# One-hot expert rows copied by ScalarE to a layout with each token's keys contiguous, for the gate matmuls' stationary side

## The chip, the core and the metric

The kernel runs on one core of a Trainium2 chip. The engines named here are TensorE (PE, whose weight loads the profile lists apart as PEld), VectorE (DVE), ScalarE (ACT), GpSimd (POOL) and SyncE (SP, which issues the large loads). Each engine works off its own instructions, and waits for others through semaphores. The metric is the device time of the whole program in microseconds (us).

## The reference, cut to what matters

A token batch of 256 rows of 1024 channels passes four layers. The first two of them (attention and others, not touched here) each end in a PEER feed-forward block, which chooses among 16,384 experts, laid out as 128 x 128 keys:

```python
def peer_ffn(h, w_pq, sub_keys, expert_down, expert_up):
    ...
        s = jnp.einsum('thpk,hpnk->thpn', q, sub_keys, ...)
        top_s, top_i = lax.top_k(s, PEER_TOPK)                     # 16 of 128, two lists per head
        ...
        best_s, best_pos = lax.top_k(cand_s..., PEER_TOPK)         # 16 experts for each of 8 heads
        gate = jax.nn.softmax(best_s, axis=-1)
        u = expert_down[experts]
        act = jax.nn.gelu(jnp.einsum('td,thkd->thk', t, u, ...))
        wgt = (gate * act).astype(t.dtype)
        return jnp.einsum('thk,thkd->td', wgt, expert_up[experts])
```

## The kernel before

The kernel gathers no experts. In `peer` it computes the activations of all 16,384 experts for all 256 tokens, multiplies them by a dense matrix of gates that is zero for experts not chosen, and multiplies the result by the whole up table.

**Units.** The down table comes as 64 loads of 1 MB, two units each, and a unit is 128 experts (one row of the 128 x 128 keys). For each unit `Stream.next` has ACT make a float32r high part (`whi`, L95, one CAST of 128x1024) and DVE the remainder (`wlo`, L100, one TENSOR_TENSOR of 128x1024); then PE runs 24 matmuls of 128x256 (`mtile`, L226). A pool holds three pairs of `whi` and `wlo`, so the cast for a unit waits until PE is through with the unit three before it. The split is written in the program two units ahead of its matmuls. After every second unit ACT applies GELU to the pair before (L971, and L974 with a product on DVE, L975, for the tokens whose gates are there already).

**Gates.** The generator `peer_select` is stepped between units by a debt counter: every unit is worth 1400, a step costs what it yields. Its first part finds the chosen experts of every token. Its second part, the **gate stage**, goes through the tokens four at a time, 64 groups per layer. The tile `w6` holds two sets `O` of three float16 planes of 128 keys x 4 tokens, the token index running fastest, so that two keys of a token lie 8 bytes apart. For a group, DVE compares a ramp with the row and column numbers of the chosen experts (L924, one-hot rows in plane 0, one-hot columns in plane 2), and one step later multiplies the one-hot columns by the two float16 parts of the gates (L928, planes 1 and 2). The contraction index on the partitions is the list of 128 chosen pairs. `gate_mm` then runs 8 matmuls of 128x128 for the group: plane 0 of a token is the stationary side, planes 1 and 2 are the moving side, and the results are the token's 128 x 128 gates in a bank of PSUM. `evac` takes an older group's bank: ACT copies the gates for the experts whose activations are still to come (L901, one or two pieces), and DVE multiplies them into the activations that are there (L904). In the program order a group is L924, a yield of 800, `evac`, L928, the matmuls of the group before, a yield of 800.

Nothing reorders the work: each engine's instructions stand in the order in which this Python code emits them. In the profile all matmuls carry L226, and the tiles `w` (w6), `bank` (PSUM), `arena` and `a` (activations, `a` also other scratch), `r` (loaded weights), `hthi` and `htlo` (the tokens) tell them apart. L888 are four float16 transposes, whose stationary and moving side both lie contiguous.

Of the kernel before, what the change touches and what calls it, by code (L numbers as in the profile page):

```python
# [12 lines left out]
OP = mybir.AluOpType  # L13
# [7 lines left out]
# columns of the per-channel vectors, [128, count] each  # L21
# [10 lines left out]
class Stream:  # L32
    """Loads run ahead in one queue, in the order of use; tiles of weights are split into two
    float32r parts a few units before they are needed."""
# [36 lines left out]
    def mark(self):  # L71
        """nothing behind this place is split before it is passed"""
        self.todo.append((None, None, None))
# [44 lines left out]
    def raw_due(self, ahead=0):  # L118
        """the next raw item was loaded in front of the tiles in use, or not far behind"""
        return self.raw_q and self.raw_q[0][2] < self.at + ahead  # L120


class Kern:
# [16 lines left out]
    def __init__(self, nc, tc, ctx, a, out):  # L140
        self.nc, self.tc, self.ctx, self.a, self.out = nc, tc, ctx, a, out
        P = lambda name, **kw: ctx.enter_context(tc.tile_pool(name=name, **kw))
        self.perm = P("perm", bufs=1)
        self.hl = P("hl", bufs=3)
        self.htp = P("ht", bufs=1)
        self.ps = P("ps", bufs=8, space=PSUM)
        self.sm = P("small", bufs=1)
        p = self.perm
        self.arena = p.tile([128, 26624], F32, name="arena")
        self.x = p.tile([128, 8, 256], F32, name="x")  # L150
        self.vec = p.tile([128, NVEC], F32, name="vec")
        self.ident = p.tile([128, 128], F32, name="ident")
        self.ones = p.tile([128, 128], F32, name="ones")
        self.adac = [p.tile([128, 48], F32, name=f"adac{i}") for i in range(4)]
        self.gs = p.tile([128, 8], F32, name="gs")
        self.epst = p.tile([128, 1], F32, name="epst")
        self.one = p.tile([128, 1], F32, name="one")
        self.zo = p.tile([128, 8], F32, name="zo")
        self.z2 = p.tile([128, 20], F32, name="z2")
        self.zr = p.tile([128, 1], F32R, name="zr")  # L160
        self.ident16 = p.tile([128, 128], F16, name="ident16")
        self.io4 = p.tile([128, 128, 4], F16, name="io4")
        # parts that change to float32r where the experts come
        self.rp = P("rp", bufs=1)
        self.a3 = self.rp.tile([128, 6144], F32, name="a3")
        self.r0 = self.rp.tile([128, 4096], F32, name="r0")
        self.r0s = [self.r0[:, :2048], self.r0[:, 2048:]]
        self.w6 = self.rp.tile([128, 1536], F32, name="w6").rearrange("p (a b) -> p a b", b=256)
        self.w6_at = 0
        self.late = False  # L170
        self.S = Stream(self, 2)
        self.slots = [self.arena[:, i * 2048:(i + 1) * 2048] for i in range(13)]
        self.ring = list(range(2, 10))
        self.reset()

# [12 lines left out]
    def reset(self, lo=20480):  # L188
        """scratch: parts of the arena that the loads leave alone"""
# [4 lines left out]
    def second(self):  # L194
        """from here on other tiles of scratch serve, and the loads have eight places"""
# [11 lines left out]
    def rounded(self):  # L207
        """float32r tiles for the experts"""
        self.a3 = None
        self.fa3 = self.rp.tile([128, 6144], F32R, name="fa3", tag="a3")  # L210
# [22 lines left out]
    def mtile(self, o, h):  # L233
        """o[128 outputs, 256 tokens] from the next unit of weights and h (d on partitions)."""
        hi, lo = self.S.next()
# [5 lines left out]
    def mtile2(self, os, h, lead=None):  # L241
        """two tiles at once, as the blocks of h come"""
# [39 lines left out]
    def gemv(self, l, m, cb, pool=0):  # L282
        """columns m, m + 1 of layer l's modulation, from the next raw item, without their bias"""
# [32 lines left out]
    def sq_mm(self, sq, ss, col, cols=8):  # L316
        """column sums of sq [128, 256], tokens on partitions, into columns col, cols + col"""
# [4 lines left out]
    def sums(self):  # L322
        """opens the sums of squares of x, tokens on partitions"""
# [4 lines left out]
    def sum_mm(self, sq, ss, k):  # L328
        """adds block k's squares [128, 256]"""
# [11 lines left out]
    def warm(self, n):  # L341
        """keeps the tensor engine's clock up while it would wait"""
# [5 lines left out]
    def warm_root(self):  # L348
        """has the table of the square root loaded"""
        self.nc.scalar.activation(self.one, self.epst, AF.Sqrt)  # L350

    def root(self, parts, n, d):
        """1 / sqrt(mean + eps) for the sums over the last axis of parts [128, n, ...]"""
# [6 lines left out]
    def spread(self, r):  # L360
        """r: for both blocks of tokens a column -> [128, 256], the same on all partitions"""
# [5 lines left out]
    def rstd(self, ss, r=None):  # L367
        """for both blocks of tokens a column of 1 / rms"""
# [6 lines left out]
    def norm(self, r, g, sc, sh, keep=None):  # L375
        """hi, lo of x * rstd * g * (1 + sc) + sh"""
# [25 lines left out]
    def lead(self, cb):  # L402
        """the first norm, two blocks at a time as the columns of their scale and shift come"""
# [31 lines left out]
    def x_step(self, ps, k, g, ss):  # L435
        """block k of x and its squares, whose sums the caller takes later"""
# [5 lines left out]
    def out_open(self):  # L442
        """x += g * (w_out^T h) with the channels of h in any order: four banks stay open"""
# [4 lines left out]
    def out_step(self, h, k, g=None):  # L448
        """one block of 128 channels of h; with g it is the last"""
# [29 lines left out]
    def add_mixer1(self, l, ada, every):  # L479
        """ada: pairs of modulation columns, their loads between those of the weights"""  # L480
# [15 lines left out]
    def mixer1(self, l, h, g, lead=None):  # L496
# [7 lines left out]
        # q and k, channels on partitions; heads c and c + 4 share a tile  # L504
# [47 lines left out]
        # v and the gating half, tokens on partitions  # L552
# [10 lines left out]
        # normalised q, k  # L563
# [46 lines left out]
        # y holds the three branches: attention 0..3, convolution 4..5, gating 6..7  # L610
# [79 lines left out]
        # group norm of the gating half  # L690
# [62 lines left out]
    def act(self, jp):  # L753
        """two activations of every token"""
# [3 lines left out]
    def up_order(self, i):  # L758
        """pairs whose room goes to the loads come first"""
# [3 lines left out]
    def add_peer_up(self, l, extra):  # L763
        """extra: modulation columns (layer, m0, n) whose loads go between"""
# [11 lines left out]
    def top16(self, src, n, val, idx, tmp):  # L776
        """top 16 of each row of src [128, cnt, n]; a generator, one step per row pair"""
# [19 lines left out]
    def peer_select(self, qT, keys, st):  # L797
        """top experts of every token and head -> gates and indices with the pairs on partitions,
        then the gate matrix of every token, multiplied into the activations."""
# [31 lines left out]
        for tb in range(2):  # L831
# [16 lines left out]
            # softmax over the 16 best, in two float16 parts of gate * 2^15  # L848
# [10 lines left out]
            # place among the candidates -> places in the two lists  # L859
# [31 lines left out]
        # gate matrices  # L891
# [18 lines left out]
        def gate_mm(O, t0):  # L910
            ps = self.bank()
            for t in range(4):
                o = ps[:, t * 128:(t + 1) * 128]
                self.mm(o, O[:, 0, :, t], O[:, 1, :, t], True, False)
                self.mm(o, O[:, 0, :, t], O[:, 2, :, t], False, True)
            pend.append((ps, t0))

        for t0 in range(0, 256, 4):
            # one-hot rows and columns, the columns times the gate's parts
# [4 lines left out]
            TX(O[:, 0::2], io, bc(0), op=OP.is_equal)  # L924
# [13 lines left out]
    def peer(self, l, h, g2, extra):  # L938
# [16 lines left out]
        # the arena is the activations' from here on  # L955
# [40 lines left out]
        # up: tokens stationary, the table moving  # L996
# [76 lines left out]
    def gla(self, h, g):  # L1073
# [16 lines left out]
        # decay  # L1090
# [22 lines left out]
        # values, tokens on partitions  # L1113
# [52 lines left out]
        def states(hd):  # L1166
            """the state after every chunk"""
# [96 lines left out]
    def softplus(self):  # L1264
        """8 softplus(-lambda) and its negative"""
# [23 lines left out]
    def lru(self, h, g):  # L1289
# [28 lines left out]
        def wgate(w, o, bn, b):  # L1318
            """a gate of half b, block-diagonal"""
# [141 lines left out]
    def route(self, h, hf, ht):  # L1461
        """combine weights, one-hot groups and ranks of the tokens inside their group"""
# [10 lines left out]
        # the tokens, rows  # L1473
# [23 lines left out]
        # top two of each group of four  # L1497
# [9 lines left out]
        # the first group with the largest sum  # L1507
# [8 lines left out]
        # tokens of the same group in front of each token; their count after the last  # L1516
# [6 lines left out]
        # rank inside the group, ties to the lower index  # L1523
# [35 lines left out]
    def experts(self, S, base, ht, w, oh, rk, g2, r, first=None, lent=()):  # L1559
        """slots base..base+127 of every group through the group's four experts"""  # L1560
# [19 lines left out]
        def gather(g2_):  # L1580
            """the tokens of two groups"""
# [46 lines left out]
        def turn(e):  # L1628
            """the hidden rows of expert e, channels on partitions"""
# [97 lines left out]
    def moe(self, l, h, hf, g2):  # L1727
# [22 lines left out]
        # groups of more than 128 tokens: their other slots  # L1750
# [14 lines left out]
def build(nc, tc, ctx, a, out, upto=99):  # L1765
# [7 lines left out]
    # modulation columns that load while the experts' second table does  # L1773
    extra = [[(0, 40, 8, "c"), (1, 0, 48, "c"), (2, 0, 24, "c2")], [(2, 24, 24, "c2"), (3, 0, 48, "c2")]]

    # the order of every load of the program
# [76 lines left out]
def _mtiles(w):  # L1853
    """[1024, N] -> [N / 256, 128, 2 * 1024]: two tiles of 128 outputs to a load."""
# [5 lines left out]
def arrays_of(inputs):  # L1860
# [39 lines left out]
    # modulation, [4 layers, 24, 128, 2 * 1024]  # L1900
    ada = np.stack([f["w_ada"][0], f["w_ada"][1], f["ada_w_2"][0], f["ada_w_2"][1]])
    A["ada"] = c(ada.transpose(0, 2, 1).reshape(4, 24, 2, 128, 1024).transpose(0, 1, 3, 2, 4).reshape(4, 24, 128, 2048))
    # attention bias by distance
# [72 lines left out]
```

## Time and profile before

| | |
|---|---|
| median of 3 runs | 2842.04 us (2841.47 to 2843.13) |
| profiled execution, from its first to its last instruction | 2840.8 us |
| PE busy | 2758.2 us (97%) |
| DVE busy | 2309.9 us (81%) |
| ACT busy | 1566.3 us (55%) |
| mean DMA rate | 232 GB/s |

The profiled execution has no clock but its own span, 2840.8 us, which is 1.2 us under the median of the timed runs. Busy time is a sum over stages with different limits. The gate stages lie from about 374 to 641 us (first layer) and 1329 to 1596 us (second layer) of the span, and their own rows tell what limits them.

### The profile page before, as it was taken

The page shows a single profiled execution, that of the slowest core. Times are in us where ns is not written, and L with a number is a line of the kernel's source. Part 1 is how long each engine was busy: PE and PEld are TensorE (multiplying, and loading weights), DVE is VectorE, ACT ScalarE, POOL GpSimd, SP SyncE. Part 2 cuts the span into 40 slices and gives each one's busy share as a digit, 9 for nine tenths or more (in the row PEclk, how much of TensorE's full clock was granted, in tenths as well). Part 3 has the DMA queues.
Part 4 walks back from the last instruction along what each step waited for, and adds up shares of the span by engine and source line. Part 5 has one row for each costly group of instructions (what it writes and reads, how often), then busy time and mean ns, then how long its engine had stood idle before and what let it go on. Part 6 is the DMA issues. An engine that isn't in the chain of part 4 may idle for free. (4 is left out here: it accounts for less than half of the span.)

```text
span 2840.8 us, 43874 instructions
## 1 busy us (share of the span) xinstructions
PE 2758.2 (97%) x17371; PEld 2485.0 (87%) x17371; DVE 2309.9 (81%) x3701; ACT 1566.3 (55%) x2250; POOL 68.1 (2%) x60
## 2 busy tenths in 40 slices
PE   6899999999999999999999999999999999989998
PEld 5799999998888889999999888888888887978886
DVE  7858988896788866698789868887479997779997
ACT  4554454434544445455444454455567786767785
POOL 3400000000000000000000000000000000000000
PEclk9899999999999989999999999999999999999998
DMA  9461544445899943335444479986249998359894
GB/s 379 187 239 58 173 164 142 142 148 198 334 405 359 334 169 136 125 120 177 135 149 136 172 260 371 357 337 227 90 161 358 342 349 303 135 184 364 326 361 159
DMA packets 93751, 658.09 MB, mean 232 GB/s; under 512 B 10932, under 2 KB 12468, under 8 KB 14808
## 3 DMA queue, kind: packets, MB, share of 16 engines
q1 hardware_dynamic: 90432, 649.44, 62.0%
q10 hardware_dynamic: 3096, 5.68, 0.6%
q8 instruction: 140, 2.29, 0.3%
q14 instruction: 83, 0.68, 0.1%
HBM read 654.03 MB, written 1.05 MB: 231 GB/s over the span
## 5 line engine op out<-in xcount | busy, mean ns | idle before, releaser
L100 DVE TENSOR_TENSOR wlo<-arena,whi 128x1024 fp32r<-128x1024 f32 x610 | 734.6, 1221 | 229.3 <-ACT whi L95 216.7
L226 PE MATMUL bank<-hthi,whi 128*128 128x256 f32 x2920 | 851.4, 292 | 17.7 <-ACT whi L95 9.5
L95 ACT CAST whi<-arena 128x1024 fp32r<-128x1024 f32 x610 | 631.7, 1044 | 386.0 <-PE bank L226 375.6
L226 PE MATMUL bank<-htlo,whi 128*128 128x256 f32 x2920 | 834.9, 286 | 4.0 <-DVE htlo L386 2.5
L226 PE MATMUL bank<-hthi,wlo 128*128 128x256 f32 x2920 | 833.3, 285 | 4.8 <-DVE wlo L100 4.7
L95 ACT CAST whi<-r 128x1024 fp32r<-128x1024 f32 x331 | 347.8, 1051 | 527.3 <-PE bank L226 514.6
L226 PEld LDWEIGHTS bank<-hthi,whi 128*128 128x128 f32 x2920 | 566.3, 194 | 30.7 <-ACT whi L95 9.8
L226 PE MATMUL bank<-whi,hthi 128*128 128x512 f32 (+1 forms) x1472 | 573.3, 389 | 2.4 <-ACT hthi L265 2.4
L226 PEld LDWEIGHTS bank<-htlo,whi 128*128 128x128 f32 x2920 | 565.1, 194 | 10.2 <-DVE htlo L386 7.9
L226 PE MATMUL bank<-wlo,hthi 128*128 128x512 f32 (+1 forms) x1472 | 571.3, 388 | 0.5 <-DVE wlo L100 0.5
L226 PE MATMUL bank<-whi,htlo 128*128 128x512 f32 (+1 forms) x1472 | 571.5, 388 | 0.2
L226 PEld LDWEIGHTS bank<-hthi,wlo 128*128 128x128 f32 x2920 | 563.9, 193 | 6.3 <-DVE wlo L100 6.1
L100 DVE TENSOR_TENSOR wlo<-r,whi 128x1024 fp32r<-128x1024 f32 x331 | 404.9, 1225 | 152.9 <-ACT whi L95 150.9
L226 PEld LDWEIGHTS bank<-whi,hthi 128*128 128x128 f32 x1472 | 276.4, 188 | 58.4 <-ACT hthi L265 2.8
L226 PEld LDWEIGHTS bank<-whi,htlo 128*128 128x128 f32 x1472 | 276.3, 188 | 57.5 <-DVE htlo L266 1.1
L226 PEld LDWEIGHTS bank<-wlo,hthi 128*128 128x128 f32 x1472 | 276.4, 188 | 56.4 <-DVE wlo L100 1.2
L292 DVE SCALAR_TENSOR_TENSOR arena<-arena 128x1024 f32<-128x1024 f32 x136 | 163.6, 1240 | 0.0
L226 PE MATMUL bank<-w 128*128 128x128 f16 x1024 | 142.0, 296 | 1.3 <-DVE w L928 1.3
L226 PE MATMUL bank<-whi,fw 128*128 128x512 f32 x360 | 121.8, 392 | 1.7 <-ACT fw L265 1.5
L904 DVE SCALAR_TENSOR_TENSOR arena<-bank,arena 128x416 f32<-128x416 f32 (+23 forms) x128 | 123.3, 963 | 0.0
L100 DVE TENSOR_TENSOR fa<-arena,fa 128x1024 fp32r<-128x1024 f32 x96 | 117.5, 1224 | 5.2 <-ACT fa L95 0.3
L95 ACT CAST fa<-arena 128x1024 fp32r<-128x1024 f32 x96 | 101.0, 1052 | 27.0 <-PE bank L226 26.7
(341 smaller groups left out, 2815.3 us busy)
## 6 DMA issues: line engine op xcount, KB each, us to landing
r<-in_pdown SPq DMA_DIRECT2D x110, 1024.0 KB, 4.8
arena<-in_pup SPq DMA_DIRECT2D x81, 1024.0 KB, 6.6
arena<-in_ada SPq DMA_DIRECT2D x72, 1024.0 KB, 7.0
arena<-in_mg SPq DMA_DIRECT2D x64, 1024.0 KB, 5.8
arena<-in_mu SPq DMA_DIRECT2D x64, 1024.0 KB, 6.0
arena<-in_md SPq DMA_DIRECT2D x64, 1024.0 KB, 6.4
r<-in_pup SPq DMA_DIRECT2D x47, 1024.0 KB, 5.7
r<-in_ada SPq DMA_DIRECT2D x24, 1024.0 KB, 6.8
```

The lines of the kernel that those rows point to most:

```text
L95: k.nc.scalar.copy(hi[:, :n], ap)
L100: self.k.nc.vector.tensor_sub(lo[:, :n], ap, hi[:, :n].bitcast(F32))
L226: self.nc.tensor.matmul(o, l, r, start=start, stop=stop)
L292: self.nc.vector.scalar_tensor_tensor(w, w, 1.0, cb, op0=OP.mult, op1=OP.mult, accum_out=o)
L904: nc.vector.scalar_tensor_tensor(o[:, :, :j - j0], p4[:, :, j0:j], 1.0 / GSC, o[:, :, :j - j0], op0=OP.mult, op1=OP.mult)
```

## The change

The one-hot rows now go to plane 1 and the columns stay in plane 2 (one TENSOR_TENSOR as before, its output now contiguous). ScalarE copies plane 1 to plane 0 and swaps the two axes, so that there each token's 128 keys lie contiguous. The gate matmuls take their stationary side from this copy. The moving side is read as before, 8 bytes from key to key. L928 overwrites plane 1, so it comes after the copy.

```diff
         def gate_mm(O, t0):
             ps = self.bank()
             for t in range(4):
                 o = ps[:, t * 128:(t + 1) * 128]
-                self.mm(o, O[:, 0, :, t], O[:, 1, :, t], True, False)
-                self.mm(o, O[:, 0, :, t], O[:, 2, :, t], False, True)
+                row = O[:, 0].rearrange("p j t -> p (j t)")[:, t * 128:(t + 1) * 128]
+                self.mm(o, row, O[:, 1, :, t], True, False)
+                self.mm(o, row, O[:, 2, :, t], False, True)
             pend.append((ps, t0))

         for t0 in range(0, 256, 4):
...
-            TX(O[:, 0::2], io, bc(0), op=OP.is_equal)
+            TX(O[:, 1:3], io, bc(0), op=OP.is_equal)
+
+            nc.scalar.copy(O[:, 0].rearrange("p j t -> p (j t)").rearrange("p (t j) -> p t j", t=4),
+                           O[:, 1].rearrange("p j t -> p t j"))
             yield self.GC
             if len(pend) == 2:
                 evac(*pend.popleft())
             TX(O[:, 1:3], O[:, 2:3].to_broadcast([128, 2, 128, 4]), bc(2), op=OP.mult)
             if last is not None:
                 gate_mm(*last)
```

The new file also leaves out comments and docstrings. In it the comparison is L925, the copy L927, the product L932, and L971, L974 and L975 become L975, L978 and L979.

What ACT has to do in the first layer where about half of the activations are there (which the trace of before runs from 439.7 us on), before; `r` holds the loaded weights, and the words in brackets are the semaphores that a row waits for:

```order
L95 CAST whi<-r_93 128x1024 [waits DVE_49,PE_49]
L971 ACTIVATE arena<-bank 128x2x204
L974 ACTIVATE gt<-bank 128x2x52 [waits DVE_49]
L901 ACTIVATE arena<-bank 128x4x34
L901 ACTIVATE a_92<-bank 128x4x24
L95 CAST whi<-r_93 128x1024 [waits DMAHW2_49,PE_49]
L901 ACTIVATE arena<-bank 128x4x34
L901 ACTIVATE a_92<-bank 128x4x24
```

The same place now:

```order
L927 COPY w_94<-w_94 128x512 [waits DVE_49,Activation_49]
L95 CAST whi<-r_93 128x1024
L975 ACTIVATE arena<-bank 128x2x204
L978 ACTIVATE gt<-bank 128x2x52 [waits Activation_49]
L901 ACTIVATE arena<-bank 128x4x34
L901 ACTIVATE a_92<-bank 128x4x24
L95 CAST whi<-r_93 128x1024 [waits DMAHW2_49,PE_49]
L927 COPY w_94<-w_94 128x512 [waits DVE_49,Activation_49]
L901 ACTIVATE arena<-bank 128x4x34
L901 ACTIVATE a_92<-bank 128x4x24
```

A copy (L927) stands ahead of a cast at the first place and ahead of the two pieces of an evacuation (L901) at the second, and each waits for DVE. Over the 64 groups of a layer, 37 copies have a cast right behind them and 27 an L901; outside the gate stages ACT's order is as it was.

DVE at the same place now:

```order
L925 TENSOR_TENSOR w_94<-io_88,TT 128x1024 [waits PE_49]
L100 TENSOR_TENSOR wlo<-r_93,whi 128x1024 [waits Activation_49]
L979 TENSOR_TENSOR arena<-arena,gt 128x2x52 [waits Activation_49]
L904 SCALAR_TENSOR_TENSOR arena<-bank,arena 128x4x70 [waits Activation_49]
L932 TENSOR_TENSOR w_94<-w_94,TT 128x1024 [waits DVE_49]
L100 TENSOR_TENSOR wlo<-r_93,whi 128x1024 [waits DMAHW2_49,PE_49,Activation_49]
L925 TENSOR_TENSOR w_94<-io_88,TT 128x1024 [waits PE_49]
L904 SCALAR_TENSOR_TENSOR arena<-bank,arena 128x4x70 [waits Activation_49]
L932 TENSOR_TENSOR w_94<-w_94,TT 128x1024 [waits DVE_49]
```

Its order is that of before (there the comparison is L924 and the product L928). Both the remainder (L100) and the evacuation (L904) wait for ACT, as they did; what has moved is what stands ahead of that on ACT.

## Rows read from the trace of the kernel before

**Rows 1.** The page's first part: busy us, share, instructions.

```profile
PE 2758.2 (97%) x17371; PEld 2485.0 (87%) x17371; DVE 2309.9 (81%) x3701; ACT 1566.3 (55%) x2250; POOL 68.1 (2%) x60
```

**Rows 2.** Busy time by engine in both gate stages: stretch, its length, PE, PEld, DVE, ACT, POOL, clock, DMA.

```profile
374.48:640.79 266.31, 266.31 (x2231) 262.93 (x2229) 227.49 (x308) 119.16 (x249) 0.00 (x0) 1.00 0.43 147
1329.50:1595.85 266.35, 266.35 (x2231) 262.95 (x2229) 227.45 (x308) 119.14 (x249) 0.00 (x0) 1.00 0.43 147
```

**Rows 3.** Waits in the first gate stage: us in total, times, longest.

```profile
ACT whi L95 <- PE bank L226: 145.4, 71, 2.6
DVE wlo L100 <- ACT whi L95: 30.8, 35, 1.9
DVE w L924 <- PE bank L226: 7.3, 16, 0.8
```

**Rows 4.** Timeline of DVE in the first gate stage: start, us, instruction.

```profile
440.79 0.69 DVE L924 TENSOR_TENSOR w<-io,TT 128x1024 f16<-128x1024 f16 x1 [0.71 <-PE bank L226]
441.40 1.22 DVE L100 TENSOR_TENSOR wlo<-r,whi 128x1024 fp32r<-128x1024 f32 x1
...
444.63 1.23 DVE L100 TENSOR_TENSOR wlo<-r,whi 128x1024 fp32r<-128x1024 f32 x1 [0.51 <-ACT whi L95]
445.77 0.69 DVE L924 TENSOR_TENSOR w<-io,TT 128x1024 f16<-128x1024 f16 x1
446.37 0.79 DVE L904 SCALAR_TENSOR_TENSOR arena<-bank,arena 128x280 f32<-128x280 f32 x1
447.08 0.68 DVE L928 TENSOR_TENSOR w<-w,TT 128x1024 f16<-128x1024 f16 x1
```

**Rows 5.** Timeline of ACT in the same stretch.

```profile
439.72 1.05 ACT L95 CAST whi<-r 128x1024 fp32r<-128x1024 f32 x1 [2.27 <-PE bank L226]
...
443.54 1.05 ACT L95 CAST whi<-r 128x1024 fp32r<-128x1024 f32 x1 [1.73 <-PE bank L226]
444.50 0.41 ACT L901 ACTIVATE arena<-bank 128x136 f32<-128x136 f32 x1
444.70 0.40 ACT L901 ACTIVATE a<-bank 128x96 f32<-128x96 f32 x1
```

**Rows 6.** Timeline near the stage's end: one row of PE, two of ACT.

```profile
632.83 1.11 PE L226 MATMUL bank<-w 128*128 128x128 f16 x8
...
636.74 1.05 ACT L95 CAST whi<-r 128x1024 fp32r<-128x1024 f32 x1 [2.22 <-PE bank L226]
637.69 0.21 ACT L901 ACTIVATE a<-bank 128x24 f32<-128x24 f32 x1
```

**Rows 7.** ACT's groups by shape: count, busy us, mean ns of one.

```profile
L265 ACT CAST hthi<-arena 128x512 fp32r<-128x512 f32 x104 | 63.9, 617 | 0.3 <-issue 0.3
...
L876 ACT COPY a<-a 128x2048 f16<-128x2048 f16 x8 | 15.1, 1890 | 0.0
...
L901 ACT ACTIVATE a<-bank 128x96 f32<-128x96 f32 x90 | 34.1, 379 | 0.0
...
L974 ACT ACTIVATE gt<-bank 128x104 f32<-128x104 f32 x2 | 0.5, 252 | 0.0
```

**Rows 8.** Gate matmuls (tile w), then transposes (L888): minimum, median, maximum in ns.

```profile
L226 PEld LDWEIGHTS <-w x1024: 112/117/138, 380.3 to 1600.9; 128*128 128x128 f16 x171
L226 PE MATMUL bank<-w x1024: 283/297/301, 380.4 to 1601.0; 128*128 128x128 f16 x171
...
L888 PEld LDWEIGHTS <-a x16: 96/98/99, 296.5 to 1329.5; 128*128 128x128 f16 x16
L888 PE MATMUL bank<-ident,a x16: 219/219/230, 296.5 to 1329.5; 128*128 128x128 f16 x16
```

**Rows 9.** Timeline of PE: the transposes, and one group of gate matmuls.

```profile
374.31 0.40 PE L888 MATMUL bank<-ident,a 128*128 128x128 f16 x4
...
443.47 1.11 PE L226 MATMUL bank<-w 128*128 128x128 f16 x8
```

**Rows 10.** Busy time by engine in the first 20 us, columns as in Rows 2.

```profile
0.00:20.00 20.00, 8.58 (x37) 8.12 (x37) 7.16 (x22) 7.46 (x14) 2.84 (x8) 1.00 0.91 356
```

## The prediction

> **What bounds the kernel now.** I read the page's first part, then the busy times of the two gate stages, since nothing outside them changes, then the waits inside one, then its timelines. Over the whole span PE is busy 97% [rows 1], and in the gate stages it never stops: 266.3 of 266.3 us in each [rows 2]. There DVE is busy 227.5 us and ACT 119.2 us. The reader is to see that DVE has only 38.8 us of idle time per layer, 0.61 us for each of the 64 groups, and where that lies: 30.8 us before the remainder L100, waiting for ACT's cast, and 7.3 us before the comparison L924, waiting for PE [rows 3]. The casts in turn wait 145.4 us for PE to free their tiles [rows 3]. So PE sets the pace, ACT follows it, and DVE follows ACT with little room. In the timeline a remainder that stands behind a comparison does not wait at all: the comparison ends at 441.48, the remainder starts at 441.40 (neighbours overlap by some 0.09 us in the records), because its cast had been done at 440.77 [rows 4, 5]. ACT could make that cast while DVE did other things. The evacuation L904 behind the comparison of 445.77 finds its two ACT pieces done, at 445.10, in the same way [rows 4, 5].
>
> **ACT keeps its order.** Near the stage's end a gate group's matmuls start at 632.83 and are over 1.11 us later; the piece of the evacuation that ACT has at 637.69 belongs to that group or an earlier one, and ACT stood idle for 2.22 us until 636.74 before the cast ahead of it [rows 6]. A ready instruction did not pass a waiting one. So a copy that waits for DVE holds back the cast behind it.
>
> **What the copy costs by itself.** The trace has no ScalarE copy of 512 float16 with 8 bytes between elements. The nearest rows are the cast of 128x512 out of SBUF, 617 ns, and the float16 copy of 128x2048, 1890 ns, which by the slope between them, 0.83 ns per element, also gives 0.62 us for 512 [rows 7]. From above: the pieces of L901 write with 1 KB between elements, and 128x96 takes 379 ns, where L974 writes 128x104 side by side in 252 ns [rows 7]; that is some 1.4 ns more per element, 0.7 us more for 512, so 1.33 us. Nothing excludes a little less than the cast's price; I know no row that shows it, and the copy of 2048 at the same slope speaks against it. I take 0.61, since the copy writes side by side and only its read is stepped.
>
> On this a page of the Trainium skill bears: "SBUF — State Buffer", section "Door 1: The DMA port swizzle", says that SBUF is read in lines of 16 bytes and that a step is free as long as two accesses fall into a line. The copy's read has two float16 to a line, so by this rule it would be 0.61 us, and the sum the one below; no run here shows it yet.
>
> **What it does to the order.** 128 copies of 0.61 us are 78 us of ACT, 39 us per layer, and ACT has 147 us idle there [rows 2], so its load is no matter. Its place is. The copy waits for the comparison, and two things on DVE stand behind it:
>
> - In 37 of the 64 groups the cast comes right behind the copy, and DVE's next instruction is the remainder that needs this cast. DVE now stands from the end of the comparison for one handover to ACT, the copy, the cast, and one handover back. A handover is 0.04 us (cast over at 444.59, remainder at 444.63 [rows 4, 5]), a cast 1.05 us, and two ACT neighbours overlap by 0.09 us (444.59 against 444.50) [rows 5]: 0.04 + 0.61 + 0.96 + 0.04 = 1.65 us. 37 of them are 61.1 us.
> - In 27 groups the evacuation follows. ACT's pieces of L901 now stand behind the copy, and L904 waits for them: 0.04 + 0.61 + pieces + 0.04. Two pieces take 0.51 us behind their neighbour (444.59 to 445.10) [rows 5]; late in the stage one piece of 0.21 is left, 0.12 behind its neighbour [rows 6]. I take 0.40 as the mean, so 1.09 us, 27 of them 29.4 us.
>
> The remainders that stand behind the product L928 don't wait any more: while their cast runs, DVE has L904 (0.79 us) and L928 (0.68 us) to do [rows 4]. The waits for PE vanish too, since PE is then ahead. L928 has to wait for the copy, but the waits above already cover that.
>
> **The sum.** DVE per layer: 227.5 of work + 61.1 + 29.4 = 318.0 us, against PE's 266.3. PE now waits for DVE and the stage takes 51.7 us longer; both layers 103.4 us. The profiled execution goes from 2840.8 to 2944.2, and 1.2 us more, as for the median now, gives 2945 us (+3.6%). The first group has no backlog yet, and the last copy of a layer lies in the open at the stage's end; the two go against each other, and I leave them at nothing. The up table's stage behind it starts later by as much as this one ends later.
>
> **The matmuls don't enter the sum.** Gate matmuls start 0.116 us apart ((1.11 - 0.297) / 7), the transposes, with both sides contiguous, 0.060 apart ((0.40 - 0.219) / 3) [rows 8, 9]. If the stationary side made all of this difference, PE would save 512 x 0.056 = 29 us per layer and need 238 us; if the moving side, which stays as it is, makes it, nothing. The weight loads themselves differ by 19 ns (117 against 98) [rows 8], which puts the truth nearer to the second. Either way PE is under DVE's 318, and the time is the same.
>
> **The rivals.**
>
> *Copy hidden, matmuls faster.* If ACT's part stayed ahead of DVE, PE would remain the bound and take its saving of up to 29 us per layer: 2842 - 58 = 2784. It decides where the new waits stay under DVE's slack of 0.61 us per group; my sum has 1.41 (90.5 / 64). Against it speaks that ACT keeps its order [rows 6] and that copy and cast alone are over 1.6 us. Chance 0.03. The Trainium skill's page "TensorE: Matmul & The Clock Gate", section "Weight-path perf modes — Fast Weight Load (FWL) and DoubleRow", says that the fast load of 128 weights that are not float32 works on packed and on stepped columns alike; by that rule this rival would end at 2842. The trace has the stepped load 19 ns longer, so it agrees only in part.
>
> *No effect.* The copy is hidden and the moving side paces the matmuls: 2842. The same condition; chance 0.03.
>
> *Waits partly covered.* If the two waits came to 1.1 us per group instead of 1.41, because pieces or casts still slip ahead, DVE would need 297.9 us, and the time would be 2905; with 0.8, 2867. Chance 0.09.
>
> *A dear copy.* Each 0.1 us on the copy counts 128 times, 12.8 us. At 1.03 it is 2999, at the upper bound of 1.33 it is 3037. For it speaks the price of L901's steps, against it that these are writes 1 KB apart. Chance 0.12 for over 0.8 us.
>
> *A lower clock.* PE would be busy 266 of 318 us in short gaps. If the granted clock fell to a mean of 0.8, between its levels of 1.2 and 2.4 GHz, PE would need 333 us per layer and bound the stage: 2976. Against it: in the first 20 us PE is busy 43% and the granted clock is 1.00 [rows 10]. Chance 0.03.
>
> **How the numbers follow.** My forecast has 0.70; its own range is 2925 to 2970 (a copy from 0.50 to 0.80, or pieces better covered). To it I add the upper half of the partly covered case and the dear copy up to 1.0 us: 2905 to 3000 holds about 0.83. The rest of the dear copy, to 3037, and all under 2905 are left out. 0.2% (5.7 us) is about what a measurement of this kernel can tell from no change. Slower: 0.70 + 0.09 + 0.12 + 0.03 = 0.94; same 0.03; faster 0.03.
>
> **What the changed profile would show.** Right: the gate stages 318 us long each; PE idle some 50 us in each, waiting for DVE's L932 and L100; the waits of L100 for ACT up from 30.8 to some 60 us, nearly all 1.6 us long; a new wait of some 29 us before L904; the casts' wait for PE gone, and ACT's copies waiting for DVE instead; the copy near 0.61 us; the stages outside unchanged. Wrong: a stage of 266 us or less with PE still full, which would mean that the cast ran ahead of the copy; or copies of over 0.8 us; or a granted clock under 1.00 in the stage.

## The result, and the profile after

The changed kernel takes 2954.51 us (median of 4 runs, 2951.92 to 2956.62), the kernel before 2841.76 us beside it (4 runs): a ratio of 1.0396, 95% interval 1.0381 to 1.0411. The forecast was 2945 us in a range of 2905 to 3000. The profiled execution has a span of 2953.3 us, 112.5 us more than before.

The page's first part, to be read beside [rows 1]:

```profile
PE 2778.5 (94%) x17371; PEld 2496.9 (85%) x17371; DVE 2307.8 (78%) x3701; ACT 1628.4 (55%) x2378; POOL 65.2 (2%) x60
```

Only ACT has more instructions, the 128 copies, and 62 us more work. PE's busy time has grown by 20 us, with as many instructions as before. Nobody's work has grown by 112 us; the engines wait. Where they do is told by the busy times of both gate stages, from the first to the last comparison (columns as in [rows 2]):

```profile
372.00:691.22 319.22, 278.78 (x2252) 270.39 (x2249) 226.77 (x308) 148.77 (x309) 0.00 (x0) 0.98 0.36 122
1383.63:1702.87 319.24, 281.25 (x2252) 273.21 (x2249) 226.86 (x308) 148.74 (x309) 0.00 (x0) 0.97 0.36 122
```

Each is 52.9 us longer than before [rows 2]. PE, which had filled its stage, is now idle for 40 us of it. DVE's work is what it was. The waits of the first stage, beside [rows 3] (us in total, times, longest):

```profile
ACT w L927 <- DVE w L925: 167.3, 62, 3.7
DVE wlo L100 <- ACT whi L95: 61.8, 36, 1.7
PE bank L226 <- DVE w L932: 39.1, 42, 1.8
...
DVE arena L904 <- ACT a L901: 30.6, 27, 1.5
```

The long list of casts that wait for PE (145.4 us before [rows 3]) is gone from the top; ACT waits in front of its copies, DVE for what stands behind them, PE for DVE. DVE's work and its two waits are 226.77 + 61.8 + 30.6 = 319.2 us: the whole stage. The chain is closed on DVE and ACT, and PE only follows. DVE's timeline at the place of [rows 4]:

```profile
447.36 0.69 DVE L925 TENSOR_TENSOR w<-io,TT 128x1024 f16<-128x1024 f16 x1
449.76 1.23 DVE L100 TENSOR_TENSOR wlo<-r,whi 128x1024 fp32r<-128x1024 f32 x1 [1.71 <-ACT whi L95]
...
453.51 0.68 DVE L925 TENSOR_TENSOR w<-io,TT 128x1024 f16<-128x1024 f16 x1
455.44 0.82 DVE L904 SCALAR_TENSOR_TENSOR arena<-bank,arena 128x280 f32<-128x280 f32 x1 [1.25 <-ACT a L901]
```

And ACT's, beside [rows 5]:

```profile
448.14 0.64 ACT L927 COPY w<-w 128x512 f16<-128x512 f16 x1 [2.71 <-DVE w L925]
448.68 1.04 ACT L95 CAST whi<-r 128x1024 fp32r<-128x1024 f32 x1
...
454.28 0.65 ACT L927 COPY w<-w 128x512 f16<-128x512 f16 x1 [2.64 <-DVE w L925]
454.84 0.40 ACT L901 ACTIVATE arena<-bank 128x136 f32<-128x136 f32 x1
455.04 0.38 ACT L901 ACTIVATE a<-bank 128x96 f32<-128x96 f32 x1
```

The two pictures of the prediction are there. The comparison ends at 448.05; copy and cast follow bare until 449.72; then the remainder runs. In the other kind the copy and both pieces stand bare between 454.19 and 455.42. ACT had been idle for 2.7 us before each of these two copies; whether cast and pieces could have run in that time is what the experiments try. The instructions on tile `w` (minimum, median, maximum in ns), beside [rows 8]:

```profile
L226 PEld LDWEIGHTS <-w x1024: 95/115/131, 377.9 to 1709.7; 128*128 128x128 f16 x171
L226 PE MATMUL bank<-w x1024: 272/294/303, 377.9 to 1709.8; 128*128 128x128 f16 x171
...
L927 ACT COPY w<-w x128: 641/649/674, 372.7 to 1703.6; 128x512 f16<-128x512 f16 x128
```

The copy takes 0.65 us, and the contiguous stationary side left the gate matmuls almost as they were.

**The end of a stage** holds the rest of the 112.5 us. PE's timeline behind the last comparison (691.22) of the first layer:

```profile
691.47 1.08 PE L226 MATMUL bank<-w 128*128 128x128 f16 x8 [0.99 <-DVE w L932]
697.35 1.09 PE L226 MATMUL bank<-w 128*128 128x128 f16 x8 [4.79 <-DVE w L932]
698.18 0.56 PE L226 MATMUL bank<-hthi,whi 128*128 128x256 f32 x1
...
702.17 0.41 PE L226 MATMUL bank<-hthi,whi 128*128 128x256 f32 x1
...
702.70 0.28 PE L226 MATMUL bank<-hthi,whi 128*128 128x256 f32 x1
```

The last groups have no unit's matmuls between them. DVE has to wait there for one more cast behind a copy, the 37th of the layer, before it comes to the last product:

```profile
693.64 1.23 DVE L100 TENSOR_TENSOR wlo<-r,whi 128x1024 fp32r<-128x1024 f32 x1 [1.71 <-ACT whi L95]
```

So PE stands for 4.79 us, and then runs its next unit with 0.41 us a matmul instead of 0.28. The busy times of that stretch show why, in the clock, the last column but two:

```profile
698.18:702.58 4.40, 4.40 (x23) 4.40 (x21) 3.80 (x7) 0.20 (x1) 0.00 (x0) 0.51 0.14 60
```

The granted clock was 0.51 there, the lower of the two levels (1.2 GHz), behind the idle time, and 0.78 to 0.79 over each layer's stretch from the last comparison to the first matmul of the up table. That stretch is 16.12 us in the first layer and 15.54 in the second, where it was 12.39 and 12.38 before (with the clock at 1.00). So 2 x 52.9 + 3.7 + 3.2 = 112.7 us of the 112.5 are found.

### The profile page after: what moved, and what is told of

Its sections match the earlier page's. It is cut to its first block, busy times and chain, and to the rows that moved or that the text cites. A ratio compares the mean times of both kernels' runs of the same rounds, so it can differ in the third digit from the quotient of the medians.

```text
span 2953.3 us, 44168 instructions
## 1 busy us (share of the span) xinstructions
PE 2778.5 (94%) x17371; PEld 2496.9 (85%) x17371; DVE 2307.8 (78%) x3701; ACT 1628.4 (55%) x2378; POOL 65.2 (2%) x60
## 5 line engine op out<-in xcount | busy, mean ns | idle before, releaser
L100 DVE TENSOR_TENSOR wlo<-arena,whi 128x1024 fp32r<-128x1024 f32 x610 | 734.8, 1221 | 228.1 <-ACT whi L95 216.8
L226 PEld LDWEIGHTS bank<-hthi,whi 128*128 128x128 f32 x2920 | 572.0, 196 | 30.8 <-ACT whi L95 10.0
L100 DVE TENSOR_TENSOR wlo<-r,whi 128x1024 fp32r<-128x1024 f32 x331 | 404.6, 1224 | 222.0 <-ACT whi L95 221.1
L927 ACT COPY w<-w 128x512 f16<-128x512 f16 x128 | 83.5, 653 | 342.0 <-DVE w L925 342.0
L226 PEld LDWEIGHTS <-w 128*128 128x128 f16 x1024 | 105.4, 111 | 105.3 <-issue 82.5
L904 DVE SCALAR_TENSOR_TENSOR arena<-bank,arena 128x416 f32<-128x416 f32 (+23 forms) x128 | 121.6, 950 | 61.2 <-ACT a L901 61.2
```

The costliest lines, as they stand in the source:

```text
L100: self.k.nc.vector.tensor_sub(lo[:, :n], ap, hi[:, :n].bitcast(F32))
L226: self.nc.tensor.matmul(o, l, r, start=start, stop=stop)
L904: nc.vector.scalar_tensor_tensor(o[:, :, :j - j0], p4[:, :, j0:j], 1.0 / GSC, o[:, :, :j - j0], op0=OP.mult, op1=OP.mult)
L927: nc.scalar.copy(O[:, 0].rearrange("p j t -> p (j t)").rearrange("p (t j) -> p t j", t=4), O[:, 1].rearrange("p j t -> p t j"))
```

## The experiments

The theory was that the copy's place in ScalarE's order costs the time: cast and pieces stand behind an instruction that waits for DVE. The rivals were the work itself (ACT's load, or the memory that it reads beside DVE) and a gain from the stationary side that the waits had hidden. Each result has the kernel before beside it, on the same chip: 2842.22 us with the first four, 2842.48 with the next four, 2839.88 with the last two. `late` and `pair` were timed in several rounds, the others are one execution each.

**The copy behind the evacuation** (`late`).

```diff
             TX(O[:, 1:3], io, bc(0), op=OP.is_equal)
-            nc.scalar.copy(...)
             yield self.GC
             if len(pend) == 2:
                 evac(*pend.popleft())
+            nc.scalar.copy(...)
             TX(O[:, 1:3], O[:, 2:3].to_broadcast([128, 2, 128, 4]), bc(2), op=OP.mult)
```

> The changed kernel with the copy written later: behind the evacuation and right ahead of the product, so that casts and pieces of L901 no longer stand behind it on ScalarE; the copy itself, its 128 times, and the contiguous stationary side stay. Theory (the place in ScalarE's queue costs the time): the copy of 0.65 us is then waited for only by the product, and by the cast behind it; the gate stages go back to about 267 us each and the time to 2842 us (2835 to 2855). Rival A (the work costs the time: 128 copies of 0.65 us, 84 us, on ScalarE or on the memory port it reads through): the time stays near 2954, above 2920 in any case. Rival B (the contiguous stationary side was worth something that the waits had hidden): with the waits gone the time falls below 2842, to 2784 if it gives all of the 0.056 us per matmul.

2837.46 us (10 runs), ratio 0.9983 (0.9974 to 0.9993). Busy times of the first stage:

```profile
372.50:637.33 264.83, 264.83 (x2231) 262.07 (x2229) 228.72 (x309) 155.44 (x312) 0.00 (x0) 1.00 0.43 148
```

And two of its waits:

```profile
ACT w L930 <- DVE w L925: 44.8, 36, 2.0
DVE wlo L100 <- ACT whi L95: 27.0, 35, 1.9
```

PE fills the stage again, the clock is 1.00, and ACT has all the work of the copies (155 us). Its copies (L930 here) still wait 44.8 us for the comparison, but nothing that DVE needs soon stands behind them: L100 waits no longer than before (30.8 us), and L904 not at all. Rival A falls. Of rival B a little is left: the stages are 1.5 and 2.0 us shorter than before, 3.5 us of the 4.8 us gained; the other 1.3 are less than the 4 us between runs of one kernel.

**The copy reads a constant** (`const`).

```diff
-                           O[:, 1].rearrange("p j t -> p t j"))
+                           self.io4.rearrange("p j t -> p t j"))
```

> The changed kernel, with the copy at its place but reading the constant ramp io4 instead of plane 1, so that it waits for nothing that VectorE does in the group (plane 0 then holds the ramp instead of one-hot rows, so the gates are other numbers). Same length, same layout, same count. Theory (what costs is that cast and pieces wait behind a copy that waits for the comparison): stage about 267 us, time 2843 us (2835 to 2860). Rival (ScalarE's extra 84 us, or two engines at the same memory, cost the time): stage near 319 us, time near 2954.

2847.41 us. At the same place, with the same length and count (median 660 ns), it costs the stage nothing:

```profile
374.14:638.97 264.83, 264.83 (x2231) 262.05 (x2229) 226.57 (x309) 154.81 (x310) 0.00 (x0) 1.00 0.43 148
```

The copies still wait here, 49.9 us in 26 times, but for PE and no longer for DVE, and that costs the stage nothing. So it is the wait for the comparison, with the order behind it. Of the 9.1 us by which the span exceeds that of `late`, 8.6 lie outside the gate stages; why was not tried.

**The copy made twice** (`twice`).

```diff
-            nc.scalar.copy(...)
+            for _ in range(2):
+                nc.scalar.copy(...)
```

> The changed kernel with the copy made twice, one right behind the other. Theory (every copy lies bare on VectorE's path): 128 more copies of 0.65 us less 0.09 us of overlap are 72 us, so 3026 (3015 to 3040), with the waits of L100 for ScalarE going from 1.71 to about 2.28 us each. Rival (part of what the stage lost is not the copy but the handovers, the clock or the lost backlog, so that copies are partly hidden): under 3000.

3034.58 us. Busy times and waits of the first stage:

```profile
374.12:732.80 358.68, 293.69 (x2252) 284.70 (x2249) 225.57 (x308) 190.14 (x372) 0.00 (x0) 0.94 0.32 109
```

```profile
DVE wlo L100 <- ACT whi L95: 84.8, 36, 2.4
...
DVE arena L904 <- ACT a L901: 48.3, 27, 2.1
```

L100 waits 84.8 / 36 = 2.36 us instead of 1.72, L904 1.79 instead of 1.13. The second copy counts in full, 0.65 us for each wait; the 0.09 us of overlap that I took off was not there (two copies together take 1.34 us in ACT's timeline, one 0.65).

**A quarter of the copy** (`short`).

```diff
-            nc.scalar.copy(O[:, 0].rearrange("p j t -> p (j t)").rearrange("p (t j) -> p t j", t=4),
-                           O[:, 1].rearrange("p j t -> p t j"))
+            nc.scalar.copy(O[:, 0].rearrange("p j t -> p (j t)")[:, :128], O[:, 1, :, 0])
```

> The changed kernel with the copy at its place but of one token's 128 keys instead of all 512 elements; all four tokens use that row as stationary side (the gates are other numbers). The run with two copies lengthened a stage by 39.4 us, 0.62 us for each of 64 groups; taken back from 319.2 us by one copy this leaves 280 us, not 265. Theory (the copy's length and, beside it, about 15 us per layer for the place alone: handovers, cast and pieces in the open): with a copy of about 0.3 us the stage is 280 + 64 x 0.3 = 299 us, the time 2913 (2895 to 2925). Rival A (the loss of 54 us over 265 is in proportion to the copy's length): 265 + 54 x 0.3 / 0.65 = 290 us, time 2894 or less. Rival B (only the wait for the comparison counts, whatever stands there): 319 us, 2954.

2911.28 us; the copy takes 304 ns. The same two views:

```profile
371.63:669.68 298.05, 273.64 (x2252) 265.97 (x2249) 227.55 (x309) 126.76 (x309) 0.00 (x0) 1.00 0.39 131
```

```profile
DVE wlo L100 <- ACT whi L95: 49.4, 36, 1.4
...
DVE arena L904 <- ACT a L901: 21.1, 27, 1.1
```

DVE's work and waits make the stage here too: 227.55 + 49.4 + 21.1 = 298.05 us (and 225.57 + 84.8 + 48.3 = 358.67 with two copies). Per wait L100 has 1.37 us and L904 0.78, each 0.35 less than with the whole copy, which is 0.345 longer. With a copy of no length 1.07 and 0.48 would be left, 51.5 us per layer, and a stage of 226.8 + 51.5 = 278 us. That is worked out, not run: some 13 us per layer are the price of the place, the rest that of the length.

**The copy one step later, ahead of the pieces only** (`mid`).

```diff
             TX(O[:, 1:3], io, bc(0), op=OP.is_equal)
-            nc.scalar.copy(...)
             yield self.GC
+            nc.scalar.copy(...)
             if len(pend) == 2:
                 evac(*pend.popleft())
```

> The changed kernel with the copy of full length one step later: behind the yield, still ahead of the evacuation. In the 37 groups of a layer with a cast, the cast now stands ahead of the copy; in every group the pieces of L901 still stand behind it. One of the two new waits is taken away, the other stays. Theory (the two waits add on VectorE, and only what exceeds PE's 265 us counts): VectorE has 227 us of work and the 31 us of waits before L904, 258 us, so PE bounds again and the time is 2837 (2832 to 2848), although the copy still waits and is still waited for. Rival (each wait costs PE its own length): the stage is 265 + 31 = 296 us, time 2899.

2846.53 us. Waits of the first stage, which is 268.62 us long:

```profile
DVE arena L904 <- ACT a L901: 31.0, 28, 1.4
ACT whi L95 <- PE bank L226: 20.8, 31, 1.3
DVE wlo L100 <- ACT whi L95: 4.8, 7, 1.4
```

The wait before L904 is as long as in the changed kernel, and the stage is only 3.8 us longer than in `late`: DVE's 227.8 us and this wait come to 259 us, which is under PE's 265. So this wait alone costs almost nothing; the two together cost what exceeds DVE's slack. The other wait alone (61.8 us, against a slack of 38.8) was not run.

**The same copy on GpSimd** (`pool`).

```diff
-            nc.scalar.copy(...)
+            nc.gpsimd.tensor_copy(...)
```

> The changed kernel with the same copy at the same place of the program, but made by GpSimd, whose queue is empty in these stages. Theory (what costs is ScalarE's queue, in which casts and pieces stand behind the copy): if GpSimd needs 1 to 1.7 us for it, as for its 128x512 (1.65 us), only the product waits for it, by up to 1 us in 27 of 64 groups, which VectorE's slack of 39 us per layer holds; stages 265 to 275 us, time 2837 to 2860. Rival A (the memory traffic of the copy beside VectorE's comparison and product costs the time): VectorE's 0.69 us grow and the time is over 2870. Rival B (a GpSimd copy of over 3 us): the product waits for it in every group, over 2920.

2835.68 us, below the range I gave. Instructions on tile `w`:

```profile
L927 POOL COPY w<-w x128: 638/662/2102, 372.5 to 1589.7; 128x512 f16<-128x512 f16 x128
```

The copy is as quick there as on ACT, waits for the same comparison, and its stages are 264.8 us. Nothing stands behind it in GpSimd's queue, and the product, which needs the copy itself, waits 1.8 us per stage for it. Rival A falls too: comparison and product take 0.69 us as before.

**What a step costs the matmuls**: the kernel before without any copy, with the stationary side contiguous (`stat`), the moving side (`mov`), or both (`both`). The edit of `mov`; `stat` has the same slice in the first operand:

```diff
-                self.mm(o, O[:, 0, :, t], O[:, 1, :, t], True, False)
-                self.mm(o, O[:, 0, :, t], O[:, 2, :, t], False, True)
+                self.mm(o, O[:, 0, :, t], O[:, 1].rearrange("p j t -> p (j t)")[:, t * 128:(t + 1) * 128], True, False)
+                self.mm(o, O[:, 0, :, t], O[:, 2].rearrange("p j t -> p (j t)")[:, t * 128:(t + 1) * 128], False, True)
```

> The kernel before, without any copy, whose gate matmuls read as stationary side 128 contiguous elements of plane 0 (a quarter of the plane instead of one token's stepped keys, so the gates are other numbers). What the contiguous stationary side is worth alone. Theory (the moving side paces the matmuls): gate matmuls still start 0.116 us apart, the weight load falls from 117 to about 95 ns, stage 266 us, time 2842 us. Rival (the stationary side paces them): 0.060 us apart, stage 238 to 244 us, time 2784 to 2796.

> The kernel before, without any copy, whose gate matmuls read as moving side 128 contiguous elements of planes 1 and 2, the stationary side stepped by 8 bytes as before (the gates are other numbers). Theory (the moving side paces): gate matmuls start about 0.060 us apart instead of 0.116; PE's work per stage falls from 266 to 238 us, VectorE has 227 and now little room, so stage about 240 to 248, time 2785 to 2806. Rival (the stationary side paces, or its load of 117 ns): still 0.116 us apart, time 2842.

> The kernel before, without any copy, whose gate matmuls read both sides as 128 contiguous elements of their planes (the gates are other numbers). What no step at all is worth. Theory (the two effects add): 23.5 + 1.5 us per stage, stages about 241 us, matmuls 0.06 us apart, time 2795 to 2803. Rival (once the moving side is contiguous the stepped weight load of 114 ns is what paces, so the two together give more): stages 238 us or less, time under 2793.

`stat` 2837.21 us, `mov` 2803.01, `both` 2793.11, the last 2 us below the range I gave. Their first stages, in this order, are 264.83, 242.83 and 241.59 us:

```profile
372.14:636.97 264.83, 264.83 (x2231) 262.07 (x2229) 227.03 (x309) 118.96 (x249) 0.00 (x0) 1.00 0.43 148
...
375.31:618.14 242.83, 242.30 (x2244) 239.33 (x2242) 225.13 (x309) 119.71 (x251) 0.00 (x0) 1.00 0.47 161
...
371.84:613.43 241.59, 240.88 (x2245) 237.84 (x2243) 224.65 (x309) 119.49 (x251) 0.00 (x0) 1.00 0.48 162
```

PE's instructions on tile `w` in `stat`:

```profile
L226 PEld LDWEIGHTS <-w x1024: 95/115/118, 378.0 to 1596.0; 128*128 128x128 f16 x171
L226 PE MATMUL bank<-w x1024: 273/294/296, 378.0 to 1596.1; 128*128 128x128 f16 x171
```

And in `mov`:

```profile
L226 PEld LDWEIGHTS <-w x1024: 110/114/151, 381.2 to 1554.1; 128*128 128x128 f16 x171
L226 PE MATMUL bank<-w x1024: 216/219/314, 381.2 to 1554.2; 128*128 128x128 f16 x171
```

A group of 8 gate matmuls takes 1.08 us in PE's timeline of `stat`, 0.64 in that of `mov`, 0.62 in that of `both`, where it was 1.11 [rows 9]:

```profile
503.53 1.08 PE L226 MATMUL bank<-w 128*128 128x128 f16 x8
...
501.70 0.64 PE L226 MATMUL bank<-w 128*128 128x128 f16 x8
...
503.65 0.62 PE L226 MATMUL bank<-w 128*128 128x128 f16 x8
```

The moving side sets the pace: (0.64 - 0.219) / 7 = 0.060 us from matmul to matmul, as for the transposes, and still (1.08 - 0.294) / 7 = 0.112 in `stat`. A contiguous stationary side saves 1.5 us per stage, the moving side 23.5, both 24.7. The weight load did not do in `stat` what I expected: its median is 115 ns, not 95 (only its minimum is), though its own operand is contiguous. In `mov` the two stages give 47 us, of which 7.4 are lost again outside them; why was not tried.

**Keys 4 bytes apart, no copy** (`pair`): the planes as two pairs of tokens.

```diff
-                self.mm(o, O[:, 0, :, t], O[:, 1, :, t], True, False)
-                self.mm(o, O[:, 0, :, t], O[:, 2, :, t], False, True)
+                side = lambda i: O[:, i, t // 2, :, t % 2]
+                self.mm(o, side(0), side(1), True, False)
+                self.mm(o, side(0), side(2), False, True)
...
-            O = self.w6[:, o:o + 3, :].bitcast(F16).rearrange("p s (j t) -> p s j t", t=4)
+            O = self.w6[:, o:o + 3, :].bitcast(F16).rearrange("p s (u j t) -> p s u j t", u=2, t=2)
...
-            A["iota4"] = c(np.broadcast_to(ar[None, :, None], (128, 128, 4))...)
+            A["iota4"] = c(np.broadcast_to(ar[None, None, :, None], (128, 2, 128, 2))...)
```

`TT` holds its numbers by groups of four tokens, and L924 and L928 get one axis more.

> The kernel before without any copy, with the planes laid out as two pairs of tokens of 128 keys x 2 tokens, so that a token's keys lie 4 bytes apart instead of 8, for both sides of the gate matmuls; the whole computation is kept. Runs so far: a contiguous stationary side saves 1.5 us per stage, a contiguous moving side 23.5 us (0.046 us per matmul). Theory A (at 4 bytes the moving side comes as fast as contiguous): matmuls start about 0.06 us apart, stages 241 to 244 us, time 2790 to 2800. Theory B (the rate goes with the step, half of the loss at half the step): stages about 253 us, time about 2818. Theory C (any step costs the same): 2842. A further price: VectorE writes and reads runs of two elements instead of four; if that costs its 128 instructions of 0.69 us per layer 10%, its 227 us become 236, still under 242.

2795.41 us (5 runs, 2792.37 to 2796.17), ratio to before 0.9833 (0.9820 to 0.9847): 1.7% under the kernel before, and with the whole computation kept. Theory A holds. Instructions on tile `w`:

```profile
L226 PEld LDWEIGHTS <-w x1024: 96/97/145, 377.9 to 1549.9; 128*128 128x128 f16 x171
L226 PE MATMUL bank<-w x1024: 217/218/308, 377.9 to 1550.0; 128*128 128x128 f16 x171
...
L926 DVE TENSOR_TENSOR w<-io,TT x128: 671/686/732, 372.1 to 1545.2; 128x1024 f16<-128x1024 f16 x128
```

Load and matmul are those of contiguous operands, within a nanosecond, and DVE's comparison takes 0.69 us as before. The busy times say what bounds the stage now:

```profile
372.08:614.53 242.45, 241.91 (x2244) 238.93 (x2242) 224.93 (x308) 119.60 (x251) 0.00 (x0) 1.00 0.47 161
```

PE still, and by only 17 us.

## Why the prediction was right

- *PE sets the pace, DVE follows with 0.61 us of slack per group.* `mid` shows that slack hold one of the two waits: 31 us are waited there, and the stage is 2.3 us longer than before (3.8 longer than in `late`).
- *ACT keeps its order; the copy holds back what stands behind it.* Shown by `late`, `const` and `pool`, which keep the copy and take away, in turn, what stands behind it, what it waits for, and the queue it stands in: the first stage is 264.8 us in all three.
- *37 waits of 1.65 us and 27 of 1.09 us.* Measured 36 of 1.72 and 27 of 1.13 within the stage, which ends where the last comparison starts; the 37th wait, of 1.71, lies behind it. The two terms were 61.1 and 29.4; like for like they are 63.5 (61.8 and 1.7) and 30.6.
- *A copy of 0.61 us.* It takes 0.65, mis-sized by 0.04 us. The 63 waits within a stage came out 3.6 us longer than 36 of 1.65 and 27 of 1.09; the copies make 2.5 of that, and DVE's own work gave back 0.7 (226.8 for 227.5). It is a little over the 0.62 of the nearest rows and far under the bound of 1.33; the dear copy did not come. *12.8 us per 0.1 us* holds: from a quarter copy to a whole one it is 43.2 us for 0.345 (12.5), and for the second copy 80.1 us for 0.65 (12.3).
- *DVE 318.0 us per stage, so 51.7 us more.* 319.2, and 52.9 more, without the 37th wait, which 318.0 held. For both layers that is 105.8 us where I had 103.4.
- *The first group and the last copy at nothing.* This term was mis-sized too: the end of a stage costs 3.7 and 3.2 us. Of each, 1.7 are the 37th wait, which the sum had counted; the rest it had not. PE has used up its backlog there, waits 4.79 us, and in the first layer runs 4.4 us at the lower clock behind it, 1.9 us of loss (20 matmuls 0.21 us apart instead of 0.12). In `late`, where PE has its backlog, the same stretch is 12.5 us. Of the 9.1 us between the sum (2944.2) and the span (2953.3), 5.7 are the stages, above all the longer copy, and 3.6 their ends beyond that wait; all else gave back 0.2.
- *Matmuls outside the sum, the truth nearer to the moving side.* Right: the stationary side is worth 1.5 us per layer of the 29 that were its bound, and the rival at 2784 had no ground even with the copy hidden, as `late` shows. `both`, with no step on either side, reaches 2793. The sign I had placed it by was no good one, though: the load's 19 ns. In `stat` the load is contiguous and still takes 115 ns, so they need not come from the stationary side's step. The reading came out right by luck, and the sum did not rest on it.
- *The clock stays.* This was wrong in the small: three stretches of 3 us in the first stage and five in the second ran at 0.50, each behind a wait of PE of 1.5 to 1.8 us, and a granted clock under 1.00 was among the signs I had named for an error. PE had the room: with these it was busy for 279 of 319 us, and so idle for 40 us where I had named some 50. In `short`, where the clock stayed at 1.00, DVE's work and waits make the stage in the same way. Only at the stage's end did the clock reach the path.

The Trainium skill's rule on lines of 16 bytes ("SBUF — State Buffer", section "Door 1: The DMA port swizzle") was taken for the copy, and the copy agrees with it within 0.04 us. Read for the moving side, it would also call the step of 8 bytes free, and there the runs say otherwise: 0.112 to 0.116 us per matmul at 8 bytes, 0.060 or less at 4 or 2; the measurement decides. Of the rule that the fast weight load works on packed and on stepped columns ("TensorE: Matmul & The Clock Gate", section "Weight-path perf modes — Fast Weight Load (FWL) and DoubleRow") the trace agrees at 4 bytes (97 ns against 98 packed); at 8 bytes the load takes 114 ns.

## What to carry to other kernels

An instruction put on an engine with 45% of its time idle can still lengthen the program, if it waits for the engine that will next need what stands behind it there: count for each group the wait, the copy and all that follows it bare, and hold that against the waiting engine's slack, not against the copying engine's idle time. Write such a copy where its input has long been ready, or on a queue with nothing behind it, and before a layout is repaired with a copy, measure which operand sets the pace. Here it was the other one, and a layout with half the step, which costs no instruction, gave nearly all of the gain.

## What the runs showed of the hardware beyond that

- The moving side of a 128x128 float16 matmul costs 0.057 to 0.060 us when its elements lie 2 or 4 bytes apart, worked out as above from the groups of `both`, `pair` (0.63 us) and `mov`, and 0.112 to 0.116 us at 8 bytes. A stationary side stepped by 8 bytes lengthens the load by 16 ns (114 in `mov` against 98 in `both`), and that hardly shows behind a moving side that is slower; a contiguous one takes 115 ns behind a moving side of 8 bytes (`stat`).
- GpSimd makes the copy with 8 bytes between the read elements in 0.66 us (median), as quick as ACT. DVE was busy 234.1 us in that stage instead of 227.0 in `stat`, where nobody copies. Most of it lies in 25 products behind GELU (L979 there, 558 ns in the mean against 333 in `stat`); why was not tried.
- ACT's price for a float16 copy of 512 elements is 0.65 us and of 128 elements 0.30 us, with a stepped read: 0.90 ns per element, where the casts and copies of [rows 7] gave 0.83.
